# Moving the subtractions that GpSimd did outside the expert stages to VectorE, in a two-block transformer kernel

## The chip, the cores and the metric

The kernel runs on one core of a Trainium2 chip. A core has five engines that run side by side, each with a queue of its own that it works off strictly in order: TensorE (PE in the profile, with PEld for the loading of its stationary operand), VectorE (DVE), ScalarE (ACT), GpSimd (POOL) and SyncE (SP, which here only issues transfers). They wait for each other by semaphores. Sixteen DMA engines move data between HBM and the on-chip memory SBUF; matrix products land in the accumulators of PSUM. The metric is the time of one execution on the device, in microseconds, lower is better.

## The reference

256 tokens of width 1024 pass through two blocks, all in float32. The lines that matter, in the order in which the kernel computes them:

```python
# first block, layer 0: mLSTM, layer 1: multi-head latent attention (MLA)
x = layer_norm(DN_ALPHA * x + mix, ln_g[i, 0], ln_b[i, 0])          # mix = mlstm_mixer or mla_mixer
x = layer_norm(DN_ALPHA * x + peer_ffn(x, ...), ln_g[i, 1], ln_b[i, 1])   # expert stage: 16384 experts, top 16 of 8 heads
x = x + sigmoid(x @ ple_w_gate[i]) * (p[i] @ ple_w_proj[i])          # gated addition ("c0", "c1" in the kernel)
...
# second block
h = modulate(rmsnorm(x, norm_mix_g[l]), sh1, sc1)
x = x + g1 * hybrid_mixer(h, ...)     # sparse attention (8 heads) + stick-breaking attention (8 heads), merged by gates
h = modulate(rmsnorm(x, norm_ffn_g[l]), sh2, sc2)
x = x + g2 * swiglu(h, ...)           # silu(h @ w_gate) * (h @ w_up) @ w_down
return rmsnorm(x, norm_final_g)
```

Inside `mlstm_mixer` the gates go through running sums and running maxima over the tokens; inside `mla_mixer` and `hybrid_mixer` there are softmax steps per head. `peer_ffn` scores all keys, takes the best 16 experts per head and token and adds up their weighted outputs.

## The kernel before

**How a product is made.** Activations lie transposed, features on the 128 partitions and the 256 tokens along the row. Each float32 product is built of three products of a shorter type, called by `mm3` (L159 to L161): every operand is cut into a high part `hi` (the value copied to the short type) and a low part `lo` (the value less `hi`). L159 multiplies hi by hi, L160 and L161 the two mixed pairs. So each weight has to be split before it can be used, and a low part is an operation with two inputs in SBUF.

**How weights come.** `prep` loads one slab of 1 MB (128 partitions x 2048 values) into one of 3 `raw` buffers by a transfer issued on SP. It is split in two halves; `split` (its two lines are L128 and L129) issues for each half a copy `hi` on ScalarE (shown under L78, the helper for all ScalarE work; 8 buffers) and a subtraction `lo` (L129; 7 buffers). The argument `lo_engine` says who does the subtraction: VectorE if it is missing, GpSimd where the caller passes `nc.gpsimd`. A `raw` buffer is free for the next transfer when both halves are split, a `lo` buffer when TensorE has done the last product that reads it. `slab` calls `prep` where that hasn't been done; `linT` and `linN` multiply by all slabs of a matrix, giving the result transposed or not.

**Who subtracted before.** In the page, 634 subtractions of weights stand on VectorE and 120 on GpSimd. Those of GpSimd are 40 in the expert stages (in `peer` and the look-ahead loads there) and 80 outside them: the value, output-gate and output matrices of the mLSTM layer (`a_w_v`, `a_w_og`, half of `a_w_out`), every second slab of the gated additions (`ple_w_gate`), the MLA projections (`mla_kn`, `mla_v`, `mla_uq`, `b_w_out`), the eight slabs of `merge`, and a few first slabs of other matrices. GpSimd also does two splits of 128x512 (`pre`), one product `trig` (L961), four masked products in the stick-breaking attention (L1302), eight additions (L1350), a scaling of 128x1024 (L435), and in `post_norm` 48 subtractions of 128x128 (L276).

**The stages**, by the time in the span of the profiled execution: mLSTM 0 to 145 us, norm and expert scoring 145 to 247, expert stage 247 to 980, gated addition c0 with its norm 980 to 1027, MLA 1027 to 1130, norm and scoring 1130 to 1210, second expert stage 1210 to 1965, c1 to 2023, hybrid attention to 2230, its output projection to 2290, feed-forward to the end.

**What sets the order.** The program is written as straight Python; a framework orders the instructions of every engine by a model of their durations, and puts in the semaphores. So where a subtraction stands in VectorE's queue is the scheduler's choice, and whatever stands behind it waits if it waits. `behind` and `issue_after` only hold pieces of work back until a named instruction is issued.

**The places named further down.** In the mLSTM layer L464 to L469 make the gates' running sums on VectorE (32x256), L481 transposes them on TensorE, and L482 copies the result. L221 to L228 (`rsqrt` by two refinement steps, tiny operands) serve every norm; L340 and L342 spread its result over the partitions. In c0 and c1, L853 and L854 form `(tanh + 1) * p` and add it to `x`; then c0 splits `x` (lines L128, L129, tile `s`) and transposes it (L871), and c1 takes squares (L320) and scaled copies (L372) for the next norm, whose sum is L330. In the MLA heads L896 to L898 make scores, softmax is L988 (maximum), an exponential on ScalarE, L993 and L995 (dividing), L1004 transposes, L905 multiplies by the values. L997 is the same step as L995 in the hybrid attention.

Of the kernel before, what the change touches and what calls it, by code (L numbers as in the profile page):

```python
# [17 lines left out]
OP = mybir.AluOpType  # L18
# [4 lines left out]
P = 128  # L23
# [324 lines left out]
class Modulated:  # L348
# [28 lines left out]
    def finish(self, name, evac):  # L377

        B, v = self.B, self.B.nc.vector
        self.rms.col()  # L380
        rs = self.rms.bc()
        ws = B.slab(name, 0, B.nc.gpsimd)
        ps = [B.psum("acc") for _ in range(2)]
        for k in range(KD):
            for j in range(2):
                B.mm3(ps[j][:, 0:S + 2], ws(k, j * P, (j + 1) * P), (self.hi[:, k, :], self.lo[:, k, :]),
                      k == 0, k == KD - 1)
        for k in range(KD):
            t = B.t(self.pool, [P, S], F32, "hm", bufs=3)
            sh = B.mod[:, self.o + k:self.o + k + 1]  # L390
            g = B.mod[:, self.o + KD + k:self.o + KD + k + 1]
            hi, lo = (a[:, k, :] for a in B.xT)
            v.scalar_tensor_tensor(t, B.x32[:, k, :], g, rs, op0=OP.mult, op1=OP.mult)
            i_act = B.act(hi, t, AF.Identity, bias=sh)
            i_dve = v.scalar_tensor_tensor(lo, t, sh, hi.bitcast(F32), op0=OP.add, op1=OP.subtract)
        B.last = (i_act.ins, i_dve.ins)
        for j in range(2):
            t = B.t(self.pool, [P, S], F32, "hm", bufs=3)
            col = B.t(B.small, [P, 1], F32, "wsh")
            v.tensor_copy(col, ps[j][:, S:S + 1])  # L400
            v.tensor_tensor(t, ps[j][:, 0:S], rs, op=OP.mult)
            evac(j, t, col)
# [11 lines left out]
def mlstm(B):  # L414
    nc, A = B.nc, B.A
    mm = nc.tensor.matmul
    v = nc.vector
    act = B.act
    with B.pool("ml") as p, B.pool("mlw", 2) as w:
        for n, i in (("a_w_gate", 0), ("a_w_qk", 0)):  # L420
            B.prep(n, i, nc.gpsimd if i else v)
        nc.sync.dma_start(B.X, A["x"])
# [61 lines left out]
        act(flo, tok[:, :, 32:40], AF.Exp, scale=-1.0)  # L484
        acc = B.linN(B.xT, "a_w_v", lo_engine=nc.gpsimd)
        for tb in range(2):
# [62 lines left out]
        for h in range(8):  # L549
            if h < 7:  # L550
                head_a(h + 1)
            for i in gates[h]:
                hf, k = i // 8, i % 8
                ws = B.slab("a_w_og", k // 4 * 2 + hf, nc.gpsimd) if k % 4 == 0 else ws
                for tb in range(2):
# [11 lines left out]
            if h in (6, 7):  # L567
                B.accN(acc, [(oT, B.slab("a_w_out", h - 6, nc.gpsimd), 2 * h - 12, 2)], h == 6, False)
        norm_heads(1)
        B.warm()  # L570
        B.accN(acc, [(oT, B.slab("a_w_out", s), 2 * s, 2) for s in (2, 3)], False, True)
        with B.pool("rows") as rows:
            B.prep("peer_w_q", 0, nc.gpsimd)
            B.post_norm(acc, 0, rows)
# [251 lines left out]
def norm_ple(B, acc, li, pre, pre_p):  # L826

    nc, A = B.nc, B.A
    v = nc.vector
    act = B.act  # L830
    with B.pool("plew", 2) as w:
# [3 lines left out]
        nc.sync.dma_start(p32, A["pT"][li])  # L835
        B.split(p32, *pT, nc.gpsimd)
        B.prep("ple_w_proj", li, nc.gpsimd)
        if acc:
# [23 lines left out]
        with B.behind():  # L862
            B.linT(B.xT, "ple_w_gate", range(li * 4, li * 4 + 4), ev, lambda s: nc.gpsimd if s % 2 else v,
                   k_outer=True, base=li * 8)
# [10 lines left out]
def mla(B):  # L875
# [5 lines left out]
    with B.pool("mla") as p, B.pool("mlaw", 2) as w, ExitStack() as ctx2:  # L881
# [44 lines left out]
        def w_out(s):  # L926
            B.accN(acc, [(oT, B.slab("b_w_out", s, nc.gpsimd), 2 * s, 2)], s == 0, False)

        with B.pool("lat") as lt:
# [26 lines left out]
            rkb = rk.bc()  # L956
            B.linT(ckT, "mla_kn", [0], lambda c, ps: v.tensor_tensor(kn[:, c, :], ps, rkb, op=OP.mult), nc.gpsimd)
            rq.col()
            rqb = rq.bc(192.0 ** -0.5)
            trig = B.t(lt, [P, S], F32, "trig")  # L960
            nc.gpsimd.tensor_tensor(trig, B.trig, rqb, op=OP.mult)  # L961
            acc = B.linN(ckT, "mla_v", nc.gpsimd)
            for tb in range(2):
# [9 lines left out]

            heads(lambda s: B.linT(cqT, "mla_uq", [s], ev_q, nc.gpsimd))
        B.warm()
        B.accN(acc, [(oT, B.slab("b_w_out", s, nc.gpsimd), 2 * s, 2) for s in (2, 3)], False, True)
        with B.pool("rows") as rows:
            B.prep("peer_w_q", 8, nc.gpsimd)
            B.post_norm(acc, 2, rows)
# [64 lines left out]
def hybrid(B):  # L1044
# [5 lines left out]
    with B.pool("hy") as p, B.pool("hyw", 2) as w, ExitStack() as es:  # L1050
# [37 lines left out]
        nc.sync.dma_start(w2, A["w2"])  # L1088
        B.linT(hT, "nsa_in", [1], ev_a, nc.gpsimd, k_outer=True)
        with B.behind():  # L1090
# [151 lines left out]
        ob = (B.t(p2, [P, 4, S], F32R, "obh"), B.t(p2, [P, 4, S], F32R, "obl"))  # L1242
        merge = lambda i: B.linT(hT, "merge", [i], lambda c, ps: v.tensor_copy(mg[:, c, :], ps), nc.gpsimd)

# [47 lines left out]
        def stick_sp(i):  # L1292
# [8 lines left out]
            for o in (0, S):  # L1301
                nc.gpsimd.tensor_tensor(ab[:, :, o:o + P], ab[:, :, o:o + P],  # L1302
                                        sm.unsqueeze(1).to_broadcast([P, 4, P]), op=OP.mult)
# [43 lines left out]
        def ev_yb(c, ps):  # L1347
            t = B.t(w, [P, S], F32, "vT")
            v.scalar_tensor_tensor(t, mg[:, 8 + c, :], 1.0, ps, op0=OP.add, op1=OP.mult)
            nc.gpsimd.tensor_tensor(t, mg[:, c, :], t, op=OP.add)  # L1350
            act(hT[0][:, c, :], t, AF.Copy, scale=0.5)
# [20 lines left out]
def ffn(B, out):  # L1372
    nc, A, v = B.nc, B.A, B.nc.vector
    with B.pool("ff") as p, B.pool("ffw", 2) as w:
# [18 lines left out]
        rms = Rms(B, p, RMS_EPS)  # L1393
        B.linT(hT, "ffn_up", [0], ev_u, nc.gpsimd, k_outer=True)
        for s in range(1, NF // 2):
# [182 lines left out]
```

## Time and profile before

| | |
|---|---|
| median of three runs | 2478.57 us (2474.83 to 2481.1) |
| the profiled execution, its own time | 2474.93 us |
| its span, first to last instruction | 2472.0 us |
| TensorE busy | 2373.6 us, 96% of the span, mean granted clock 0.981 |
| VectorE busy | 1627.4 us, 66% |
| ScalarE busy | 1230.4 us, 50% |
| GpSimd busy | 346.4 us, 14% in 212 instructions |

Busy time counts what an engine executes, from the start to the end that the profiler recorded. It does not tell waiting inside an instruction from working: an instruction that is held up while it runs has a longer duration, and looks busy. So durations of the same operation and shape are to be compared with each other. "Idle before" is time in which the engine stood still, and the releaser is what ended it. A granted clock of 1.00 is 2.4 GHz, 0.50 is 1.2 GHz.

### The profile page before, as it was taken

What the parts mean: (1) busy time and instruction counts of PE and PEld (TensorE: products, weight loads), DVE (VectorE), ACT (ScalarE), POOL (GpSimd) and SP (SyncE); (2) the same over time, 40 slices, a digit from 0 to 9 for tenths busy, and PEclk for the clock granted to TensorE, in tenths of its full rate; (3) what the DMA queues carried; (4) which work ended last, traced back from release to release, by engine and by line L of the source; (5) the groups of instructions that cost most, each with busy time, mean ns of one, the idle gap of its engine ahead of it and who ended that gap; (6) DMA issues with size and microseconds to landing.
All of it is one profiled execution on the core that took longest, in us unless ns stands there. A gap on an engine that the chain in (4) does not pass through costs nothing. (4 is left out here: it accounts for less than half of the span.)

```text
span 2472.0 us, 40796 instructions
## 1 busy us (share of the span) xinstructions
PE 2373.6 (96%) x16430; PEld 2167.0 (88%) x16430; DVE 1627.4 (66%) x3069; ACT 1230.4 (50%) x1813; POOL 346.4 (14%) x212
## 2 busy tenths in 40 slices
PE   7989999999999999989989999999999989999998
PEld 6779898889999998978989888999999888789998
DVE  5469995786666665656999566555555573459554
ACT  5455555444444444645455444444444464455442
POOL 5345000000000001445300000000000131313000
PEclk9989999999999999999999999999999999999999
DMA  7334577887677664433367766656655344224543
GB/s 258 120 110 150 226 282 268 293 326 264 251 263 273 255 227 148 154 137 131 144 239 280 258 236 218 227 200 208 218 208 201 137 162 160 81 86 161 198 149 108
DMA packets 134204, 495.22 MB, mean 200 GB/s; under 512 B 8064, under 2 KB 76032, under 8 KB 80896
## 3 DMA queue, kind: packets, MB, share of 16 engines
q1 hardware_dynamic: 129120, 458.55, 51.8%
q10 hardware_dynamic: 4896, 34.08, 3.4%
q8 instruction: 128, 2.10, 0.3%
q14 instruction: 60, 0.49, 0.1%
HBM read 457.99 MB, written 34.60 MB: 199 GB/s over the span
## 5 line engine op out<-in xcount | busy, mean ns | idle before, releaser
L78 ACT ACTIVATE hi<-raw 128x1024 fp32r<-128x1024 f32 (+1 forms) x754 | 771.3, 1044 | 838.8 <-PE ps L160 336.8
L129 DVE TENSOR_TENSOR lo<-raw,hi 128x1024 fp32r<-128x1024 f32 (+1 forms) x634 | 778.0, 1234 | 420.6 <-PE ps L161 254.2
L159 PE MATMUL ps<-s,hi 128*128 128x256 f32 x3248 | 923.5, 285 | 16.3 <-ACT hi L78 13.8
L160 PE MATMUL ps<-s,hi 128*128 128x256 f32 x3248 | 924.2, 285 | 2.1 <-DVE s L276 1.5
L161 PE MATMUL ps<-s,lo 128*128 128x256 f32 x3248 | 921.0, 284 | 5.3 <-DVE lo L129 5.3
L159 PEld LDWEIGHTS ps<-s,hi 128*128 128x128 f32 x3248 | 617.4, 190 | 22.6 <-ACT hi L78 14.2
L160 PEld LDWEIGHTS ps<-s,hi 128*128 128x128 f32 x3248 | 618.3, 190 | 7.4 <-issue 2.2
L161 PEld LDWEIGHTS ps<-s,lo 128*128 128x128 f32 x3248 | 617.9, 190 | 7.3 <-DVE lo L129 7.3
L129 POOL TENSOR_TENSOR lo<-raw,hi 128x1024 fp32r<-128x1024 f32 (+1 forms) x120 | 292.4, 2455 | 1340.6 <-ACT hi L78 1148.9
L159 PE MATMUL acc<-hi,ah 128*128 128x512 f32 x1024 | 400.6, 391 | 9.6 <-ACT ah L78 9.5
L160 PE MATMUL acc<-lo,ah 128*128 128x512 f32 x1024 | 401.0, 392 | 0.0
L161 PE MATMUL acc<-hi,al 128*128 128x512 f32 x1024 | 400.1, 391 | 0.0
L159 PEld LDWEIGHTS acc<-hi,ah 128*128 128x128 f32 x1024 | 193.1, 189 | 49.1 <-ACT ah L78 10.8
L161 PEld LDWEIGHTS acc<-hi,al 128*128 128x128 f32 x1024 | 193.0, 189 | 41.2 <-DVE al L129 0.7
L160 PEld LDWEIGHTS acc<-lo,ah 128*128 128x128 f32 x1024 | 193.0, 188 | 37.9
L129 DVE TENSOR_TENSOR al<-aw,ah 128x512 fp32r<-128x512 f32 x128 | 88.2, 689 | 54.9 <-ACT ah L78 54.8
L78 ACT ACTIVATE ah<-aw 128x512 fp32r<-128x512 f32 x128 | 80.1, 626 | 71.3 <-DVE aw L789 62.5
L789 DVE TENSOR_TENSOR aw<-g,wt 128x256 f32<-128x256 f32 x156 | 59.3, 422 | 39.4 <-ACT g L78 39.4
L756 PE MATMUL ps<-oh,o 128*128 128x128 f16 x512 | 65.1, 219 | 11.5 <-DVE oh L750 5.0
L78 ACT ACTIVATE st<-ps 128x512 f32<-128x512 f32 x128 | 66.6, 604 | 1.6 <-ACT pre L78 1.6
L78 ACT ACTIVATE g<-ps 128x512 f32<-128x512 f32 (+1 forms) x82 | 46.5, 567 | 39.1 <-PE ps L161 39.1
L757 PE MATMUL ps<-ol,o 128*128 128x128 f16 x512 | 64.7, 218 | 0.0
(461 smaller groups left out, 2433.6 us busy)
## 6 DMA issues: line engine op xcount, KB each, us to landing
raw<-in_peer_u SPq DMA_DIRECT2D x128, 1024.0 KB, 4.9
raw<-in_peer_v SPq DMA_DIRECT2D x128, 1024.0 KB, 4.9
wd<-st ACTq DMA_DIRECT2D x32, 1024.0 KB, 4.5
wt<-wd SPq DMA_DIRECT2D x32, 1024.0 KB, 6.1
raw<-in_w_ada SPq DMA_DIRECT2D x24, 1024.0 KB, 5.3
raw<-in_peer_w_q SPq DMA_DIRECT2D x16, 1024.0 KB, 4.9
raw<-in_ffn_gate SPq DMA_DIRECT2D x11, 1024.0 KB, 4.8
raw<-in_ffn_up SPq DMA_DIRECT2D x11, 1024.0 KB, 4.8
```

Source lines behind the costliest of these rows:

```text
L78: i = self.nc.scalar.activation(out, in_, func, **kw)
L129: (lo_engine or self.nc.vector).tensor_tensor(lo, src, hi.bitcast(F32), op=OP.subtract)
L159: mm(out, lhsT[0], rhs[0], start=first, stop=False)
L160: mm(out, lhsT[0], rhs[1], start=False, stop=False)
L161: mm(out, lhsT[1], rhs[0], start=False, stop=last)
L756: mm(ps[:, i * P:(i + 1) * P], o2[:, t // 2, :, t % 2], oh1[:, t // 2, :, t % 2], start=True, stop=False)
L757: w_last = mm(ps[:, i * P:(i + 1) * P], o2[:, t // 2, :, t % 2], ol1[:, t // 2, :, t % 2], start=False, stop=True)
L789: v.tensor_tensor(aw[:, sl].rearrange("p (g t) -> p g t", t=16), g[:, sl].rearrange("p (g t) -> p g t", t=16), wt[:, :, (j % 4) * 2 + i, : ...
```

## The change

Wherever a caller outside the expert stages asked for GpSimd, the argument is dropped, so that VectorE does the subtraction; the operations on GpSimd at L961, L1302 and L1350 are issued on VectorE too. GpSimd keeps what `peer` and its look-ahead give it, the 48 operations of `post_norm` (L276), the scaling at L435, and masks and counters that read nothing. The diff, cut to its core (`prep`, `slab`, `linT`, `linN` and `split` are the same as before):

```diff
-        ws = B.slab(name, 0, B.nc.gpsimd)
+        ws = B.slab(name, 0)
...
-            B.prep(n, i, nc.gpsimd if i else v)
+            B.prep(n, i)
...
-        acc = B.linN(B.xT, "a_w_v", lo_engine=nc.gpsimd)
+        acc = B.linN(B.xT, "a_w_v")
...
-                ws = B.slab("a_w_og", k // 4 * 2 + hf, nc.gpsimd) if k % 4 == 0 else ws
+                ws = B.slab("a_w_og", k // 4 * 2 + hf) if k % 4 == 0 else ws
...
-                B.accN(acc, [(oT, B.slab("a_w_out", h - 6, nc.gpsimd), 2 * h - 12, 2)], h == 6, False)
+                B.accN(acc, [(oT, B.slab("a_w_out", h - 6), 2 * h - 12, 2)], h == 6, False)
...
-            B.prep("peer_w_q", 0, nc.gpsimd)
+            B.prep("peer_w_q", 0)
...
-        B.split(p32, *pT, nc.gpsimd)
-        B.prep("ple_w_proj", li, nc.gpsimd)
+        B.split(p32, *pT)
+        B.prep("ple_w_proj", li)
...
-            B.linT(B.xT, "ple_w_gate", range(li * 4, li * 4 + 4), ev, lambda s: nc.gpsimd if s % 2 else v,
+            B.linT(B.xT, "ple_w_gate", range(li * 4, li * 4 + 4), ev,
                    k_outer=True, base=li * 8)
...
-            B.linT(ckT, "mla_kn", [0], lambda c, ps: v.tensor_tensor(kn[:, c, :], ps, rkb, op=OP.mult), nc.gpsimd)
+            B.linT(ckT, "mla_kn", [0], lambda c, ps: v.tensor_tensor(kn[:, c, :], ps, rkb, op=OP.mult))
...
-            nc.gpsimd.tensor_tensor(trig, B.trig, rqb, op=OP.mult)
-            acc = B.linN(ckT, "mla_v", nc.gpsimd)
+            v.tensor_tensor(trig, B.trig, rqb, op=OP.mult)
+            acc = B.linN(ckT, "mla_v")
...
-            heads(lambda s: B.linT(cqT, "mla_uq", [s], ev_q, nc.gpsimd))
+            heads(lambda s: B.linT(cqT, "mla_uq", [s], ev_q))
...
-        merge = lambda i: B.linT(hT, "merge", [i], lambda c, ps: v.tensor_copy(mg[:, c, :], ps), nc.gpsimd)
+        merge = lambda i: B.linT(hT, "merge", [i], lambda c, ps: v.tensor_copy(mg[:, c, :], ps))
...
-                nc.gpsimd.tensor_tensor(ab[:, :, o:o + P], ab[:, :, o:o + P],
+                v.tensor_tensor(ab[:, :, o:o + P], ab[:, :, o:o + P],
...
-            nc.gpsimd.tensor_tensor(t, mg[:, c, :], t, op=OP.add)
+            v.tensor_tensor(t, mg[:, c, :], t, op=OP.add)
```

The same argument also goes at `b_w_out` (four slabs), `peer_w_q` slab 8, `nsa_in` slab 1 and `ffn_up` slab 0. In all, 80 weight subtractions (72 of 128x1024, 8 of 128x768) and 15 other operations change their engine. In numbers: 22 of the subtractions lie in the mLSTM layer, 28 in c0 and MLA, 10 in c1, 20 in the hybrid attention and after it.

Where they stand now is the scheduler's doing. First VectorE's queue in the mLSTM layer, where the gates' running sums end (`lo_497` to `lo_565` are low parts of `a_w_v`, `tok` the copies after the transposes of L481):

```order
 L468 TENSOR_TENSOR Bc_240<-Bc_240,M_243 32x256
 L469 COPY ab_48_238<-Bc_240 32x256
+L129 TENSOR_TENSOR lo_497<-raw_494,hi_496 128x1024
+L129 TENSOR_TENSOR lo_501<-raw_494,hi_500 128x1024
+L129 TENSOR_TENSOR lo_531<-raw_528,hi_530 128x1024
+L129 TENSOR_TENSOR lo_535<-raw_528,hi_534 128x1024
+L129 TENSOR_TENSOR lo_565<-raw_562,hi_564 128x1024
 L482 COPY tok_481<-ps_482 128x64
 L482 COPY tok_481<-ps_485 128x64
```

Five of the subtractions stand behind the last step of the running sums and ahead of the copies; none stands among the steps themselves.

Second VectorE's queue in MLA, ahead of the heads, where the norm of the query latents is finished (`lo_11000` and `lo_11111` are low parts of `mla_uq`, 128x768):

```order
 L957 TENSOR_TENSOR kn_10452<-ps_10744,rsk_10687 128x256 x2
+L129 TENSOR_TENSOR lo_11000<-raw_10993,hi_10999 128x768
 L221 TENSOR_SCALAR rmqh_10765<-ps_10759 128x2
 L222 RECIPROCAL rmq_10764<-rmq_10764 128x2
+L129 TENSOR_TENSOR lo_11111<-raw_11108,hi_11110 128x768
 L226 TENSOR_TENSOR rmqh_10765<-rmqh_10765,rmq_10764 128x2
 L227 TENSOR_TENSOR rmqh_10765<-rmqh_10765,rmq_10764 128x2
 L228 SCALAR_TENSOR_TENSOR rmq_10764<-rmqh_10765,rmq_10764 128x2
 L340 TENSOR_SCALAR dgq_10772<-ident_79,rmq_10764 128x128 x2
```

Here a subtraction now stands in the middle of the chain that ends in L340.

Third VectorE's queue in c1, among the gate steps (`lo_20472` to `lo_20584` and `lo_20700` belong to `ple_w_gate` and the first slabs of the hybrid attention):

```order
+L129 TENSOR_TENSOR lo_20472<-raw_20469,hi_20471 128x1024
 L372 SCALAR_TENSOR_TENSOR s_3196_20235<-x_17_117,mod_108,s_3195_20234 128x256
 L320 TENSOR_TENSOR sqs_20302<-sqs_20302,sq_20310 128x256
 L372 SCALAR_TENSOR_TENSOR s_3196_20235<-x_17_117,mod_108,s_3195_20234 128x256
+L129 TENSOR_TENSOR lo_20476<-raw_20469,hi_20475 128x1024
+L129 TENSOR_TENSOR lo_20580<-raw_20577,hi_20579 128x1024
 L853 SCALAR_TENSOR_TENSOR sg_20374<-sg_20374,pre_1862_11564 128x256
 L853 SCALAR_TENSOR_TENSOR sg_20383<-sg_20383,pre_1862_11564 128x256
 L854 TENSOR_TENSOR x_17_117<-x_17_117,sg_20374 128x256
 L854 TENSOR_TENSOR x_17_117<-x_17_117,sg_20383 128x256
+L129 TENSOR_TENSOR lo_20584<-raw_20577,hi_20583 128x1024
 L320 TENSOR_TENSOR sqs_20302<-sqs_20302,sq_20378 128x256
```

Subtractions now stand between the pairs of gate steps. SP's queue of transfers is the same in both kernels.

## Rows read from the trace of the kernel before

**Rows 1.** The page: busy time, share of the span, instructions of each engine.

```profile
PE 2373.6 (96%) x16430; PEld 2167.0 (88%) x16430; DVE 1627.4 (66%) x3069; ACT 1230.4 (50%) x1813; POOL 346.4 (14%) x212
```

**Rows 2.** Instructions of L129: duration in ns min/median/max, first and last start, forms.

```profile
L129 DVE TENSOR_TENSOR lo<-raw,hi x634: 818/1225/3425, 10.6 to 2448.5; 128x1024 fp32r<-128x1024 f32 x151, 128x768 fp32r<-128x768 f32 x8
...
L129 POOL TENSOR_TENSOR lo<-raw,hi x120: 1795/2403/3930, 35.4 to 2257.6; 128x1024 fp32r<-128x1024 f32 x112, 128x768 fp32r<-128x768 f32 x8
...
L129 DVE TENSOR_TENSOR s<-x,s x16: 409/422/2591, 5.2 to 1026.1; 128x256 fp32r<-128x256 f32 x16
```

**Rows 3.** Waits of PE over the run: us in total, times, longest us.

```profile
PE acc L159 <- ACT s L78: 5.2, 1, 5.2
...
PE acc L871 <- DVE x L854: 3.8, 2, 2.1
...
PE ps L481 <- POOL lo L129: 3.4, 1, 3.4
PE ps L330 <- DVE sqs L320: 3.1, 2, 2.9
PE ps L342 <- DVE dgq L340: 2.9, 1, 2.9
...
PE ps L896 <- ACT e L78: 2.3, 1, 2.3
PE ps L540 <- ACT sg L78: 2.3, 1, 2.3
PE ps L905 <- ACT pT L78: 2.1, 2, 1.7
```

**Rows 4.** Stretches: length, busy PE, PEld, DVE, ACT, POOL, PEclk, DMA share, GB/s.

```profile
930.00:1150.00 220.00, 201.19 (x1318) 181.68 (x1318) 131.12 (x244) 117.97 (x222) 84.22 (x58) 0.95 0.36 131
```

**Rows 5.** Timeline, mLSTM gates: start us, us, engine, line, out<-in [idle before <-releaser].

```profile
36.43 0.67 DVE L464 TENSOR_TENSOR_SCAN Bc<-lf,zero 32x256 f32<-32x256 f32 x1
37.14 2.44 DVE L465 TENSOR_TENSOR ab<-ig,Bc 32x256 f32<-32x256 f32 x1
39.61 2.77 DVE L467 TENSOR_TENSOR_SCAN M<-ab,zero 32x256 f32<-32x256 f32 x1
...
44.88 2.31 DVE L469 COPY ab<-Bc 32x256 f32<-32x256 f32 x1
```

**Rows 6.** Timeline of POOL, 35 to 53 us.

```profile
35.37 18.75 POOL L129 TENSOR_TENSOR lo<-raw,hi 128x1024 fp32r<-128x1024 f32 x7 [5.70 <-DVE lf L458]
```

**Rows 7.** The stretch right after PE's wait at L481, columns as in Rows 4.

```profile
47.70:51.10 3.40, 3.40 (x9) 2.66 (x10) 0.23 (x2) 2.11 (x3) 3.40 (x2) 0.50 0.82 299
```

**Rows 8.** Timeline of DVE, 128 to 136 us.

```profile
132.64 2.32 DVE L227 TENSOR_TENSOR hrh<-hrh,hr 128x8 f32<-128x8 f32 x1
```

**Rows 9.** Timeline of DVE, end of c0.

```profile
1021.63 2.59 DVE L129 TENSOR_TENSOR s<-x,s 128x256 fp32r<-128x256 f32 x1
```

**Rows 10.** Timeline of DVE and ACT, norm ahead of the MLA heads.

```profile
1056.31 1.72 DVE L227 TENSOR_TENSOR rmqh<-rmqh,rmq 128x2 f32<-128x2 f32 x1
...
1056.50 0.83 ACT L78 ACTIVATE hi<-raw 128x768 fp32r<-128x768 f32 x1
```

**Rows 11.** Timeline of DVE, MLA heads.

```profile
1073.03 2.07 DVE L995 TENSOR_SCALAR e<-e,sm 128x256 f32<-128x256 f32 x1
...
1078.99 0.36 DVE L995 TENSOR_SCALAR e<-e,sm 128x256 f32<-128x256 f32 x1
```

**Rows 12.** Timeline of DVE, c1.

```profile
1996.18 4.05 DVE L853 SCALAR_TENSOR_TENSOR sg<-sg,pre 128x256 f32<-128x256 f32 x2 [1.65 <-ACT sg L78]
2000.15 2.95 DVE L854 TENSOR_TENSOR x<-x,sg 128x256 f32<-128x256 f32 x2
...
2012.95 0.75 DVE L853 SCALAR_TENSOR_TENSOR sg<-sg,pre 128x256 f32<-128x256 f32 x2
```

**Rows 13.** Waits of POOL, 1062 to 1130 us, columns as in Rows 3.

```profile
POOL lo L129 <- PE ps L161: 9.8, 5, 4.4
```

**Rows 14.** Waits of POOL, 2060 to 2230 us.

```profile
POOL lo L129 <- PE ps L161: 101.5, 9, 57.0
```

More of the change, by code (lines that the diff above doesn't have):

```diff
@@ L926, in w_out @@
         def w_out(s):
-            B.accN(acc, [(oT, B.slab("b_w_out", s, nc.gpsimd), 2 * s, 2)], s == 0, False)
+            B.accN(acc, [(oT, B.slab("b_w_out", s), 2 * s, 2)], s == 0, False)
         with B.pool("lat") as lt:
@@ L972, in ev_q @@
                 v.tensor_tensor(qn[c // 4][:, c % 4, :], ps, trig if c % 2 else rqb, op=OP.mult)
-            heads(lambda s: B.linT(cqT, "mla_uq", [s], ev_q, nc.gpsimd))
+            heads(lambda s: B.linT(cqT, "mla_uq", [s], ev_q))
         B.warm()
-        B.accN(acc, [(oT, B.slab("b_w_out", s, nc.gpsimd), 2 * s, 2) for s in (2, 3)], False, True)
+        B.accN(acc, [(oT, B.slab("b_w_out", s), 2 * s, 2) for s in (2, 3)], False, True)
         with B.pool("rows") as rows:
-            B.prep("peer_w_q", 8, nc.gpsimd)
+            B.prep("peer_w_q", 8)
             B.post_norm(acc, 2, rows)
@@ L1088, in hybrid @@
         nc.sync.dma_start(w2, A["w2"])
-        B.linT(hT, "nsa_in", [1], ev_a, nc.gpsimd, k_outer=True)
+        B.linT(hT, "nsa_in", [1], ev_a, k_outer=True)
         with B.behind():
@@ L1393, in ffn @@
         rms = Rms(B, p, RMS_EPS)
-        B.linT(hT, "ffn_up", [0], ev_u, nc.gpsimd, k_outer=True)
+        B.linT(hT, "ffn_up", [0], ev_u, k_outer=True)
         for s in range(1, NF // 2):
```

## The prediction

> **What bounds the kernel now.** First the engine line [rows 1]: TensorE is busy for 2373.6 of the 2472.0 us of the span, VectorE for 66%, GpSimd for 14%. So the end is set by TensorE, and a change on other engines counts only where TensorE stands still for them, or runs at half clock after standing still. All of its idle time is 98.4 us. Then the waits of TensorE [rows 3], which are the places where something can be won. Eight of them lie in stages where GpSimd subtracts: L481 3.4, L540 2.3, L871 3.8 (two waits), L342 2.9, L896 2.3, L905 2.1, L159 behind a scaled copy 5.2, L330 3.1; together 25.1 us. All are for VectorE or for ScalarE behind it, but for L481, where the view names GpSimd.
>
> Then the durations, since a busy VectorE may be a held-up one. In the mLSTM layer a running sum of 32x256 takes 0.67 us at 36.43, and the running maximum of the same size 2.77 at 39.61; the steps around it, no larger, take 2.44 and 2.31 [rows 5]. GpSimd is subtracting without a pause from 35.37 to 54.1 [rows 6]. The same shows everywhere: L227 on 128x8 takes 2.32 [rows 8], a split of 128x256 2.59 [rows 9] with a median of 0.42 over 16 [rows 2], L995 2.07 and six us later 0.36 [rows 11], a pair of L853 4.05 and later 0.75 [rows 12]. The long ones are as long as one subtraction on GpSimd, whose median is 2.40 [rows 2]: the two engines do not share, one is shut out until the other has finished. It goes both ways, GpSimd's longest subtraction is 3.93 and VectorE's 3.42 [rows 2].
>
> The Trainium skill says the same on "SBUF — State Buffer", § Who interferes with whom: an instruction of VectorE with two inputs in SBUF is locked out for the whole of a GpSimd instruction that reads SBUF, and the other way round, by who begins first; the rows above agree.
>
> **The change part by part.**
>
> What moves: 80 weight subtractions. On VectorE the median is 1.225 us [rows 2], so 72 of 128x1024 cost 88 us; the 8 of 768 take about three quarters, 0.9 each, 7 us. The 15 others, by their sizes, come to some 9 us. So VectorE gets about 104 us of work. What goes are the held-up instructions. Each costs about what [rows 8, 9, 11, 12] show, 1.7 to 2.2 us more than its own time; I count some fifty in the trace, the first of them at 37.14 [rows 5], 80 us in all, of which about 70 in the stages where the change takes GpSimd's work away. So VectorE's busy time rises by only some 30 us, to about 1660, and in place of long steps there are short ones with subtractions between them. In total that is little; what counts is which stand ahead of the steps that TensorE waits for.
>
> A. L481 (wait 3.4). The chain of the four steps ends at 44.88 + 2.31 = 47.19 [rows 5]. Free of GpSimd each takes at most the 0.67 of the first, so from 37.14 it ends by 39.8, before TensorE comes to the transposes (47.3 less the wait of 3.4, 43.9). The five subtractions stand behind the chain and not in it; they end by 39.8 + 5 x 1.22 = 45.9, and for each of them TensorE has twelve products of 512 columns to do, of which nine took 3.40 us at half clock [rows 7], so at least 2.3 at full clock; the other subtractions follow in time. The whole wait goes, and no later step takes its place. Behind it TensorE ran 3.40 us at half clock, busy all the time [rows 7]; with no idle stretch ahead I count that back too, 1.7. **-5.1 us**, bounds -3.4 and -5.1.
>
> B. L540 (2.3). L227 loses 2.15. But `lo_1229` now stands between L226 and L227 and costs 1.22, and it waits for a `lo` buffer that TensorE is reading until about then. L226 comes earlier, since the first step of that chain was held up too. **-1.1**, bounds 0 and -2.3.
>
> C. L871 in c0 (3.8). Of the second wait (2.1) the 2.59 for a split of 0.42 [rows 9] is the whole cause. The first hangs on a ScalarE copy whose load came late, since its `raw` buffer was kept by a subtraction on GpSimd (2.4 instead of 1.2). The gated slabs' four subtractions join VectorE's queue ahead of the pairs L853, L854; one waits for a `lo` buffer. I take three quarters, -3, and 1 for half clock behind it. **-4**, bounds -1 and -5.5.
>
> D. L342 (2.9). L227 loses 1.5 [rows 10]. But `lo_11111` stands between L222 and L226 now, 0.96 us long, and its high part comes from ScalarE only at 1056.50 + 0.83 = 1057.33 [rows 10], behind a copy there that itself waits for TensorE. So L226 starts at 1058.3 and L340 ends where it did or later. **+0.5**, bounds -1.5 and +1.2.
>
> E. MLA heads, L896 and L905 (4.4 in all). Both waits end behind an L995 held up by 1.7 [rows 11]. Eleven subtractions (13 us) enter the queue here, against about 11 us of hold-ups that go, and some stand right ahead of an L993 or L995. **-2**, bounds -4.4 and +4.
>
> F. c1, L159 and L330 (5.2 and 2.9 in one row). From 1996 the pairs take 4.05 and 2.95 instead of 0.75 each [rows 12], the next pair of L853 again some 4; with the two subtractions before them (one of 3.42) that is about 11.5 us of hold-ups. Eight subtractions enter ahead of the last pair, 9.8 us, of which some 4 fit where VectorE stood idle for ScalarE (1.65 before the pair, [rows 12], once more before the next). 11.5 - 5.8 = 5.7 at best; two copies now stand in ScalarE's queue behind a load, so I take **-4.4**, bounds -1 and -8 (with clock, -9).
>
> G. Nothing for the rest. Hybrid attention: three held-up L997 go, 16 subtractions come; TensorE's waits there sum to under 4 us in the whole stage, since its many small products keep it busy, so 0, bounds -2 and +3. Output projection and feed-forward: TensorE has no wait of a us that ends with VectorE; its cover is TensorE's own work of 256-column products, and gone it would cost the eight L1350 at some 0.4 each, 3 us. `pre` and `trig` lie where VectorE idles. Expert stages and `post_norm` are as before. Transfers start a little earlier, as `raw` buffers come free in 1.2 instead of 2.4 us; TensorE does not wait for loads in these stages, so 0.
>
> Sum: -5.1 - 1.1 - 4 + 0.5 - 2 - 4.4 = **-16.1 us**. The profiled execution took 2474.93 us (span 2472.0 and 2.9 around it), so 2458.8. It lies at the low end of the three runs; from the median of 2478.57 the same sum gives 2462.5. I say 2460.
>
> A rule that speaks against the change is in the Trainium skill, "Perfetto Trace Analysis", § Optimizing Scalar/DVE Operations: where VectorE is saturated, giving work to GpSimd may make sense. By it VectorE would become the bound; the share in [rows 4], 131.12 of 220 us, is 60%, part of it waiting, so the row does not show the saturation that it asks for. The same section adds that it may not help between these two engines because of the shared port, which is what the durations above show.
>
> **The rivals.**
>
> 1. *The queue takes back what the lock gives.* VectorE works strictly in order; wherever a subtraction stands ahead of a step that TensorE waits for, 1.2 us of it replace 1.7 to 2.1 of hold-up. Then only A and B remain, with D against them, and C, E, F are zero: -5.7, or 2469 to 2473. For it: eleven, eight and four subtractions enter E, F, C. Against: half of them fit in VectorE's idle time.
>
> 2. *Slower: VectorE inherits GpSimd's waits for `lo` buffers.* GpSimd stood 9.8 us in five waits for TensorE to release a buffer in the MLA heads [rows 13] and 101.5 in nine in the hybrid attention [rows 14], with nobody behind it. On VectorE the softmax steps stand behind such a wait. If the 9.8 and the shorter five of the nine (14 us in sum) reach TensorE, they take back 23.8, +7.7 net: about 2483 to 2486. It decides from the point where a subtraction is queued more than a us before its buffer is released and L988 or L995 is next. For it: `lo` has 7 buffers, all full there. Against: the scheduler places the subtractions late, after several steps of a head.
>
> 3. *More comes back.* If the waits of C, E and F go whole and TensorE keeps full clock behind them, -5.1 - 2.3 - 5.5 - 4.4 - 9 = -26: 2449 to 2452.
>
> 4. *It isn't GpSimd that holds VectorE up.* Then the long durations stay, 104 us are added, and A gets 6 us longer: about 2485. Against: each long step lies beside a GpSimd instruction and none without one.
>
> **How the numbers follow.** Forecast 0.54, rival 1 0.19, rival 2 0.10, rival 3 0.14, rival 4 0.03. A measurement of this kernel tells some 0.3% (7.4 us) from no change. Against the median that is 2471.1: the forecast and rival 3 lie below, and of rival 1 about a quarter; faster 0.73. Same 0.16: the rest of rival 1 and the mild end of rival 2. Slower 0.11. The range leaves out rivals 2 and 4 and the far end of 3: 2449 to 2475.
>
> **What would show it.** In the profile after: four steps L464 to L469 under 0.7 us each and no wait at L481; no L853, L995 or L227 over 1 us outside the expert scoring; subtractions on GpSimd 40; VectorE busy 1640 to 1680; the waits of L871 and of L159 for a scaled copy under 1 and 4 us; L342's wait about 3. The prediction is wrong if new waits of TensorE for L988, L995 or L997 appear behind subtractions that wait for TensorE (rival 2), or if TensorE's idle time stays near 98 us while the steps are short (rival 1).

## The result and the profile after

The changed kernel takes 2439.2 us (median of 6 runs, 2436.3 to 2447.5), the kernel before in the same series 2479.84: ratio 0.9842, 95% interval 0.982 to 0.9864, some 40 us or 1.6% less. In a second series it took 2442.68 against 2478.72, 0.9852 (0.9833 to 0.9872). The direction was as forecast, the size was not: the prediction's sum was 16.1 us and its time 2460 us, and 2439 lies 10 us below the low end of the range.

The engine line of the page of the changed kernel, against [rows 1], and the L129 rows of the view by lines, against [rows 2] (duration in ns min/median/max):

```profile
PE 2354.2 (97%) x16430; PEld 2152.7 (88%) x16430; DVE 1655.3 (68%) x3164; ACT 1231.7 (51%) x1813; POOL 134.2 (6%) x117
```

```profile
L129 DVE TENSOR_TENSOR lo<-raw,hi x714: 820/1225/3409, 10.1 to 2410.9; 128x1024 fp32r<-128x1024 f32 x169, 128x768 fp32r<-128x768 f32 x10
...
L129 POOL TENSOR_TENSOR lo<-raw,hi x40: 2368/2398/3372, 156.6 to 1182.9; 128x1024 fp32r<-128x1024 f32 x40
L129 DVE TENSOR_TENSOR s<-x,s x16: 417/422/428, 5.0 to 1010.4; 128x256 fp32r<-128x256 f32 x16
```

80 subtractions are gone from GpSimd, and VectorE is busy for 28 us more, not for the 104 us of its new work: the rest was made up of instructions that had been held up. The split `s`, which had a maximum of 2.59 us, now has one of 0.43. The gates' chain shows the same (timeline of VectorE, against [rows 5]): 0.67, 0.41, 0.68, 0.41 and 0.28 us, done at 39.3 instead of 47.2. The copy L469 has a single input and was held up like the others (2.31 us, now 0.28), and so was L995 with one tensor and one value per partition [rows 11]; so it was not only steps with two inputs. Of the steps of VectorE that take over 1 us more than the median of the same operation and shape in the changed kernel, the kernel before has 39 and the changed one 4, all subtractions in the expert scoring, where GpSimd still works.

```profile
36.73 0.67 DVE L464 TENSOR_TENSOR_SCAN Bc<-lf,zero 32x256 f32<-32x256 f32 x1
37.44 0.41 DVE L465 TENSOR_TENSOR ab<-ig,Bc 32x256 f32<-32x256 f32 x1
37.88 0.68 DVE L467 TENSOR_TENSOR_SCAN M<-ab,zero 32x256 f32<-32x256 f32 x1
...
39.04 0.28 DVE L469 COPY ab<-Bc 32x256 f32<-32x256 f32 x1
```

TensorE's waits over the whole run (us in total, times, longest), against [rows 3]. Of the 25.1 us of eight waits four small ones are left; L481, L896, L330 and the 5.2 us at L159 no longer appear.

```profile
PE ps L342 <- DVE dgq L340: 2.1, 1, 2.1
...
PE ps L905 <- ACT pT L78: 1.2, 1, 1.2
PE ps L540 <- ACT sg L78: 1.1, 1, 1.1
...
PE acc L871 <- DVE x L854: 0.2, 1, 0.2
```

That is 20.5 us, and the span is shorter by 37.7. Where the other half is can be read from windows that are cut at the same products of both kernels (columns as in [rows 4]: length, busy PE, PEld, DVE, ACT, POOL with counts, granted clock, DMA). First the kernel before: mLSTM; c0 with the beginning of MLA; the heads; c1; the hybrid attention with its output projection.

```profile
0.00:151.01 151.01, 130.83 (x658) 105.74 (x658) 76.56 (x171) 75.50 (x127) 61.13 (x36) 0.95 0.47 169
...
982.80:1055.48 72.68, 65.71 (x501) 63.46 (x499) 45.01 (x82) 50.01 (x95) 36.84 (x26) 0.95 0.40 145
1055.48:1129.37 73.89, 66.38 (x388) 56.37 (x386) 39.47 (x93) 31.20 (x71) 29.12 (x15) 0.95 0.32 114
...
1967.19:2021.80 54.61, 43.30 (x309) 42.30 (x307) 38.80 (x67) 33.29 (x72) 28.35 (x29) 0.84 0.42 156
2021.80:2272.82 251.02, 244.97 (x1724) 213.37 (x1723) 146.48 (x315) 130.66 (x253) 64.18 (x33) 0.97 0.33 120
```

The same five in the changed kernel:

```profile
0.00:140.35 140.35, 123.56 (x657) 100.35 (x658) 85.41 (x193) 75.54 (x127) 6.56 (x14) 1.00 0.49 182
...
972.16:1039.84 67.68, 64.25 (x501) 62.38 (x499) 49.27 (x95) 50.43 (x95) 5.58 (x12) 0.97 0.43 156
1039.84:1108.85 69.01, 65.69 (x388) 56.14 (x386) 41.24 (x107) 31.39 (x71) 0.24 (x1) 0.95 0.34 123
...
1946.58:1989.24 42.66, 39.44 (x309) 38.54 (x307) 33.94 (x75) 33.37 (x72) 6.94 (x21) 0.96 0.47 177
1989.24:2235.26 246.02, 240.32 (x1724) 210.49 (x1723) 157.55 (x347) 131.05 (x253) 0.34 (x1) 0.99 0.34 126
```

The stages are shorter by 10.7, 5.0, 4.9, 12.0 and 5.0 us, 37.5 in sum; the windows left out, with the expert stages, norms and feed-forward, differ by 0.14 us at most. Idle time of TensorE (length less busy) falls by 3.4, 3.5, 4.2, 8.1 and 0.4 us, 19.6 in sum. Its busy time falls as well, by 7.3, 1.5, 0.7, 3.9 and 4.7 us, 17.9 in sum, with as many products. Products that take less time with the same shapes are products at a higher clock, and the column of the granted clock says so in four of the five: 0.95 to 1.00, 0.95 to 0.97, 0.84 to 0.96, 0.97 to 0.99. So about half of this profile's gain is time that TensorE no longer waits, and half is clock. The prediction had 13.4 for the one and 2.7 for the other. How much of this belongs to this one profile is taken up below.

### The profile page after: what moved, and what is told of

Read it like the earlier page. It is cut to its first block, busy times and chain, and to the rows that moved or that the text cites. A ratio compares the mean times of both kernels' runs of the same rounds, so it can differ in the third digit from the quotient of the medians.

```text
span 2434.3 us, 40711 instructions
## 1 busy us (share of the span) xinstructions
PE 2354.2 (97%) x16430; PEld 2152.7 (88%) x16430; DVE 1655.3 (68%) x3164; ACT 1231.7 (51%) x1813; POOL 134.2 (6%) x117
## 4 chain that ended last, share of the span: by engine, by line
PE 47%; DVE 1%; ACT 1%; DMA 1%; issue 0%; DVEq 0%; SPq 0%; ACTq 0%
PE ps L160 9%; PE ps L161 9%; PE ps L159 9%; PE acc L159 5%; PE acc L160 5%; PE acc L161 5%; PE ps L1258 1%; PE acc L1271 0%; DMA wt<-wd 0%; PE ps L756 0%; PE acc L1144 0%; DVE lo L129 0%; PE ps L757 0%; PE ps L1259 0%; PE ps L1004 0%
## 5 line engine op out<-in xcount | busy, mean ns | idle before, releaser
L129 DVE TENSOR_TENSOR lo<-raw,hi 128x1024 fp32r<-128x1024 f32 (+1 forms) x714 | 865.4, 1219 | 456.6 <-PE ps L161 269.5
L159 PE MATMUL ps<-s,hi 128*128 128x256 f32 x3248 | 921.5, 285 | 15.9 <-ACT hi L78 13.3
L159 PEld LDWEIGHTS ps<-s,hi 128*128 128x128 f32 x3248 | 615.4, 190 | 22.1 <-ACT hi L78 13.7
L159 PE MATMUL acc<-hi,ah 128*128 128x512 f32 x1024 | 401.1, 392 | 10.3 <-ACT ah L78 10.2
L159 PEld LDWEIGHTS acc<-hi,ah 128*128 128x128 f32 x1024 | 193.4, 189 | 49.6 <-ACT ah L78 11.5
L160 PEld LDWEIGHTS acc<-lo,ah 128*128 128x128 f32 x1024 | 193.2, 189 | 37.7
L129 DVE TENSOR_TENSOR al<-aw,ah 128x512 fp32r<-128x512 f32 x128 | 88.3, 690 | 55.4 <-ACT ah L78 54.6
L276 POOL TENSOR_TENSOR s<-x,s 128x128 fp32r<-128x128 f32 x48 | 24.3, 520 | 1545.9 <-ACT x L78 1533.2
L129 POOL TENSOR_TENSOR lo<-raw,hi 128x1024 fp32r<-128x1024 f32 x40 | 98.3, 2476 | 23.4 <-PE ps L161 12.8
```

Of the source, the lines that this page charges most:

```text
L129: (lo_engine or self.nc.vector).tensor_tensor(lo, src, hi.bitcast(F32), op=OP.subtract)
L159: mm(out, lhsT[0], rhs[0], start=first, stop=False)
L160: mm(out, lhsT[0], rhs[1], start=False, stop=False)
L276: lo = (v if tb and k % 2 == 0 else nc.gpsimd).tensor_tensor(xT[1][:, k, ts], x32[:, k, ts], xT[0][:, k, ts].bitcast(F32), op=OP.subtract)
```

## Experiments

**Is it the lock, or only the quicker subtraction?** Theory A: a GpSimd operation that reads SBUF shuts VectorE out. Rival B: 1.22 instead of 2.40 us a subtraction is the gain. Two kernels have the subtractions on VectorE and then let GpSimd work beside it for nothing; in one it reads, in the other it mostly writes. They differ from the kernel before in this (`in_peer` is true inside `peer`):

```diff
-        (lo_engine or self.nc.vector).tensor_tensor(lo, src, hi.bitcast(F32), op=OP.subtract)
+        g = self.nc.gpsimd
+        beside = lo_engine is g and not self.in_peer
+        (self.nc.vector if beside else lo_engine or self.nc.vector).tensor_tensor(lo, src, hi.bitcast(F32), op=OP.subtract)
+        if beside:
+            l = lo.bitcast(F32)
```

In dve_pool_read this is followed by an operation of the same size into a spare buffer `scr`:

```diff
+            o = self.scr[:, 0:l.shape[1] * l.shape[2]].rearrange("p (k n) -> p k n", n=l.shape[2])
+            g.tensor_tensor(o, l, l, op=OP.subtract)
```

In dve_pool_write by a copy of one column and zeros:

```diff
+            g.tensor_copy(self.scr[:, 0:1], l[:, 0, 0:1])
+            for _ in range(3):
+                g.memset(self.scr[:, 0:896], 0.0)
```

L961, L1302, L1350 and the split of 128x512 stand on VectorE in both, and `hi` has 7 buffers instead of 8. The twelve subtractions of c0 and c1 stayed on GpSimd in both, other than the expectation says, since these stages are called from within `peer`; 68 of the 80 were moved and shadowed.

> All subtractions and the other moved operations stand on VectorE as in the changed kernel, but after each of the moved weight subtractions GpSimd reads the low part twice and writes the difference to a buffer that nobody uses (80 operations of the size of the old ones; 7 hi buffers instead of 8 to make room). Theory A (a GpSimd operation that reads SBUF shuts VectorE out, and TensorE waits for the held-up steps): some 30 or more steps of VectorE again over 1 us longer than their own time, VectorE busy 60 us or more above the changed kernel's 1655, the waits at L871 and at L159 for a scaled copy back, 2460 to 2485 us. Rival B (the gain is that a subtraction takes 1.22 instead of 2.40 us, so that low parts and raw buffers are ready earlier): the subtractions are as fast as in the changed kernel, 2436 to 2446 us.

Measured: 2474.8 us, ratio to the kernel before 0.9992 (0.9984 to 1.0001).

> The same as dve_pool_read, with the same order on VectorE, ScalarE and TensorE, but GpSimd copies one element per partition and then writes zeros three times (128x896), as long in sum and with hardly any reading. Theory A: few held-up steps, 2436 to 2448 us, and at least 15 us below dve_pool_read. Rival B: as dve_pool_read, both within 5 us. Rival C (any work of GpSimd hinders VectorE): as slow as dve_pool_read, both over 2460.

Measured: 2449.71 us, ratio 0.9889 (0.9873 to 0.9905). The first line below is the engine line of dve_pool_read, the second that of dve_pool_write, each from its page.

```profile
PE 2369.8 (96%) x16430; PEld 2164.6 (88%) x16430; DVE 1702.2 (69%) x3152; ACT 1234.6 (50%) x1813; POOL 311.8 (13%) x197
```

```profile
PE 2367.1 (97%) x16430; PEld 2161.6 (88%) x16430; DVE 1646.6 (67%) x3152; ACT 1235.0 (50%) x1813; POOL 363.2 (15%) x401
```

GpSimd is busier in the second, and the second is 25 us faster. VectorE executes the same 3152 instructions in both, and is busy for 55.6 us more where GpSimd reads; both traces have the mean clock 0.982, and their spans differ by 21.0 us (2472.6 and 2451.6), so the clock is not the difference there. By the count used above, 45 steps of VectorE are held up in the first and 10 in the second, these ten all in c0, c1 and the expert scoring, where GpSimd still subtracts. In c1 the pairs of L853 (here on lines 867 and 868, since lines were added) take 2.45 us beside a reading GpSimd and 0.75 beside a writing one (timeline of VectorE of the first, then of the second):

```profile
1996.07 2.45 DVE L867 SCALAR_TENSOR_TENSOR sg<-sg,pre 128x256 f32<-128x256 f32 x2
```

```profile
1991.39 0.75 DVE L868 SCALAR_TENSOR_TENSOR sg<-sg,pre 128x256 f32<-128x256 f32 x2
```

Rival B falls, though not by the total alone: in the mLSTM layer of dve_pool_read fifteen subtractions on VectorE are held up themselves (1.8 to 2.9 us). In the MLA heads eleven of twelve are as quick as in the changed kernel, and yet the stage takes 74.8 us beside a reading GpSimd and 69.5 beside a writing one, against 73.9 in the kernel before and 69.0 in the changed one (windows, cut at the same products as above, of the first and of the second):

```profile
1046.88:1121.66 74.78, 65.40 (x387) 55.23 (x386) 51.53 (x107) 32.29 (x72) 24.90 (x15) 0.95 0.31 115
```

```profile
1049.13:1118.62 69.49, 64.50 (x388) 54.88 (x386) 45.27 (x107) 32.20 (x72) 39.63 (x56) 0.98 0.34 124
```

Rival C falls too, that any work of GpSimd hinders. dve_pool_write lies just above the range expected by theory A, 9 to 12 us slower by the ratios than the changed kernel. That fits the twelve subtractions that stayed on GpSimd, the single-element copies and the buffer less; which of them it is wasn't tried apart.

**Does the clock fall because TensorE stood still?** Theory D. In the kernel before, TensorE waits 3.4 us at L481 and then runs 3.4 us at half clock [rows 7]. fill_l481 leaves the wait and fills it:

```diff
-            ps = B.psum()
+            ps = B.psum(); [mm(ps[:, P:2 * P], B.ident_b, B.cmask_b, start=True, stop=True) for _ in range(0 if tb else 56)]
             nc.tensor.transpose(ps[:, :64], ab2[:, tb * P:(tb + 1) * P], B.ident[:64, :64])
```

> The kernel before with 56 products of 128 columns, whose result is overwritten, ahead of the transposes of L481, where TensorE waits 3.4 us. They take 56 x 0.056 = 3.1 us, less than the wait, so the wait's end stays where it is. Theory D (the clock falls because TensorE stood still): no half clock at 47.7 to 51.1, the end 1.7 us earlier, or more if the later stretch at 75 goes too. Rival E (half clock comes from elsewhere): half clock stays there, the time as before, 2480.

Measured: 2475.43 us, ratio 0.9987 (0.9977 to 0.9998). The windows of its trace at the place of [rows 7] (the first us still holds the last of the additional products), and further on:

```profile
47.70:51.10 3.40, 3.40 (x31) 2.89 (x29) 1.12 (x3) 1.77 (x2) 3.40 (x3) 1.00 0.48 157
75.00:81.80 6.80, 6.80 (x19) 4.75 (x19) 0.61 (x2) 0.47 (x2) 0.58 (x2) 0.54 0.32 135
```

The clock stays at 1.00 behind the filled wait, and the gain of 2.7 us (interval 0.5 to 5.7) agrees with 1.7. But this place alone shows nothing: in only_hybrid and only_c0_mla, described below, the mLSTM code is that of the kernel before, TensorE waits 3.2 us at L481 with no filling, and the clock behind is 1.00 as well (windows right behind the wait, of the one and of the other):

```profile
48.30:51.70 3.40, 3.40 (x15) 2.80 (x16) 0.28 (x2) 2.12 (x3) 3.40 (x2) 1.00 0.82 284
```

```profile
49.40:52.80 3.40, 3.40 (x15) 2.77 (x16) 0.25 (x2) 2.12 (x3) 3.40 (x2) 1.00 0.83 296
```

In these two traces and in that of fill_l481 a stretch of 3.4 us at half clock stands at 26 to 27 us, where the first profile of the kernel before has none. The half clock at 75 stays; no wait of a us stands ahead of it, and it follows small products (L499 to L501, on 8 and 64 partitions). So there are half-clock stretches that no wait explains, and waits that none follows.

The same was tried on the changed kernel, at the four layer norms (L263) and ahead of the second half of each expert stage (L765):

```diff
-                ps[tb, h] = self.psum()
+                ps[tb, h] = self.psum(); [nc.tensor.transpose(ps[tb, h][:, 0:P], Y[:, 0, 7 * P:8 * P], self.ident) for _ in range(22 if tb and not h else 0)]
```

fill_both has this as well:

```diff
-        acc = [[B.psum("acc") for _ in range(2)] for _ in range(2)]
+        acc = [[B.psum("acc") for _ in range(2)] for _ in range(2)]; [nc.tensor.transpose(acc[0][0][:, 0:P], pre[NPRE - 2][:, 0:P], B.ident) for _ in range(36)]
```

> The changed kernel, with 22 additional transposes of 128x128 (their result is overwritten) in each of the four layer norms, between the transposes of the first and the second half of the tokens, where TensorE waits 2.8 to 3.1 us for VectorE (L260). 22 x 0.11 = 2.4 us, so they fit. In the changed kernel 6.8, 3.4, 6.8 and 3.4 us at half clock follow these waits. Theory D (half clock follows standing still, and costs half of its length): the waits stay as long, but the clock behind them is 1.00, 8 to 10 us less than the changed kernel's 2439: 2429 to 2432. Rival E (the clock falls there for another reason): half clock stays, 2438 to 2442.

Measured: 2436.86 us, ratio 0.9831 (0.9817 to 0.9844).

> As fill_norm2, and 36 such transposes (4.0 us) ahead of the second half of each expert stage, where TensorE waits 6.0 and 4.5 us for a transfer; there 6.8 and 3.4 us at half clock follow. Theory D: 3 to 5 us less than fill_norm2, 2424 to 2428. Rival E: as the changed kernel, or slower by what of the transposes doesn't fit.

Measured: 2432.73 us, ratio 0.9826 (0.981 to 0.9841). To see it beside the changed kernel, both ran once more on one chip:

> The changed kernel itself, beside fill_both_again on the same chip. Theory D says that about half of its gain is clock: mean granted clock 0.986 to 0.990 in every run against 0.977 to 0.983 of the kernel before, 2436 to 2447 us, though the profiled execution may show other stretches at half clock than the first one did, some of them in the mLSTM layer, where the first had none. If the clock of the first profile was luck, the clocks spread down to 0.982 and the median is 2445 or more.

Measured: 2442.68 us (2439.46 to 2446.68), clocks 0.985 to 0.988.

> The kernel of fill_both once more, beside the changed kernel. Theory D: 4 to 8 us less than after_again and a clock at least 0.002 higher. If the additional transposes cost what the clock gives: within 3 us of after_again.

Measured: 2435.54 us (2431.93 to 2436.37), clocks 0.990 to 0.993, 7.1 us below the changed kernel beside it; ratio to the kernel before 0.9824 (0.981 to 0.9838). Its interval overlaps that of after_again by a little, but in the two series together eight of its ten runs lie below all ten of the changed kernel. It is the fastest version here, and does nothing but more work.

The clock behind the norms, in the changed kernel and in fill_norm2 (windows):

```profile
143.60:150.40 6.80, 5.79 (x25) 5.24 (x26) 5.17 (x16) 6.13 (x16) 3.33 (x9) 0.50 0.00 0
976.50:979.90 3.40, 3.40 (x18) 3.40 (x18) 2.23 (x8) 2.90 (x9) 2.38 (x6) 0.50 0.00 0
```

```profile
145.00:152.00 7.00, 5.29 (x40) 4.33 (x39) 5.65 (x18) 6.92 (x21) 3.48 (x9) 1.00 0.00 0
976.00:983.00 7.00, 6.64 (x51) 5.63 (x50) 4.89 (x15) 6.88 (x17) 2.96 (x6) 1.00 0.01 2
```

At the third norm 3.4 of the 6.8 us stay in fill_norm2, at the fourth none. Added up over 20 us from the first transposes of each of the four norms, the twelve traces without this filling have 20 to 27 us at half clock, the three with it 3.4, 6.8 and 6.8. So at these places theory D is shown. In the whole time less came of it: 2 and 7 us where 8 to 10 and 11 to 15 were expected, and fill_norm2 alone can't be told from the changed kernel. Other half-clock stretches had come up, in fill_norm2 at 70 and at 132 us, where the code is that of the changed kernel. The second profile of the changed kernel itself shows two there as well. Its span and mean clock, and its engine line, against those of the first profile (2434.3 us, 0.989, PE 2354.2):

```profile
core 0: 2442.4 us, clock 0.985
```

```profile
PE 2362.3 (97%) x16430; PEld 2159.3 (88%) x16430; DVE 1655.4 (68%) x3164; ACT 1232.0 (50%) x1813; POOL 134.2 (5%) x117
```

The same program, the same waits of L342, L905 and L540, and 8.1 us longer; TensorE's busy time is longer by the same 8.1 us, and no other engine's by more than 0.3. Where half clock falls changes from run to run. The five windows, cut at the same products, in the second profile:

```profile
0.00:145.64 145.64, 129.78 (x657) 105.78 (x658) 84.98 (x193) 75.38 (x127) 6.67 (x14) 0.95 0.49 175
...
981.22:1048.57 67.35, 63.96 (x501) 62.12 (x499) 49.31 (x95) 50.57 (x95) 5.58 (x12) 0.97 0.43 157
1048.57:1114.98 66.41, 63.09 (x388) 53.65 (x386) 41.24 (x107) 31.40 (x71) 0.24 (x1) 1.00 0.35 127
...
1951.89:1994.52 42.63, 39.26 (x308) 38.36 (x307) 33.94 (x75) 33.38 (x72) 6.92 (x21) 0.96 0.48 178
1994.52:2243.34 248.82, 243.11 (x1725) 212.54 (x1723) 157.83 (x347) 131.14 (x253) 0.35 (x1) 0.97 0.34 125
```

Against the kernel before, TensorE's idle time falls by 20.4 us here and by 19.6 in the first profile: that part is steady. The busy time falls by 12.0 instead of 17.9; the mLSTM layer is 5.4 us shorter and not 10.7, c1 again 12.0. The first profile of the changed kernel was a lucky one, the lowest of its six runs.

**Do the stages add up?** Four kernels make the change in one stage each.

> The kernel before with the change in the mLSTM layer alone (22 subtractions: a_w_qk's, a_w_v, a_w_og, a_w_out, peer_w_q slab 0). If the stages add up, it gains what the changed kernel's trace had gained by the norm after this layer: about 10 us, so 2468; by the prediction's sum for this layer alone 6. If a gain in one stage is given back in the next, under 3.

Measured: 2466.34 us, ratio 0.9954 (0.9938 to 0.997).

> The kernel before with the change in c0 and MLA alone (28 subtractions, one split of 128x512, trig). Adding up: about 10 us, so 2468; by the prediction's terms C, D, E 5.5. If VectorE's queue takes it back there: 0 to 2.

Measured: 2463.72 us, ratio 0.9931 (0.9909 to 0.9954).

> The kernel before with the change in c1 and the first slabs of the hybrid attention alone (10 subtractions, one split). Adding up: about 11 us, so 2467; by the prediction's term F 4.4.

Measured: 2465.38 us, ratio 0.9942 (0.9926 to 0.9958).

> The kernel before with the change in the hybrid attention and after alone (20 subtractions: merge, first slabs of the feed-forward; L1302 and L1350). Adding up: about 5 us, so 2473; by the prediction 0. If what the changed kernel won there was only where its half-clock stretches fell, the gain is within 2 us of nothing.

Measured: 2474.85 us, ratio 0.9988 (0.9971 to 1.0005), not to be told from no change.

By the ratios the gains are 11.4, 17.1, 14.4 and 3.0 us; their sum of 46 is as much as the 36 to 40 of the whole change, given that each is uncertain by 4 to 6. So the stages add up within this, and rival 1 of the prediction, by which C, E and F come to nothing, falls. Only only_c0_mla gained clearly more than was expected (10). In only_c1 the stage itself is within a us of the changed kernel's, 43.65 us instead of 54.61, with 3.2 us instead of 11.3 of idle time, though the whole run's clock is only 0.980:

```profile
1978.66:2022.31 43.65, 40.42 (x309) 39.71 (x307) 33.96 (x75) 33.55 (x72) 6.93 (x21) 0.92 0.47 173
```

Each stage stands in its old form in five of the traces (the kernel before, fill_l481 and three of these four) and in its new form in five others (the two profiles of the changed kernel, peer_dve, norm_dve and the fourth). Cut at the same products, in us:

| stage | length, old form | length, new form | of it at half clock, old | new |
|---|---|---|---|---|
| mLSTM | 151.0 to 154.3 | 139.5 to 145.6 | 13.7 to 17.1 | 0 to 13.7 |
| c0, start of MLA | 72.7 to 75.3 | 67.3 to 67.7 | 6.8 to 13.7 | 3.4 |
| MLA heads | 73.7 to 74.1 | 66.4 to 69.1 | 6.8 | 0 to 6.8 |
| c1 | 54.2 to 54.6 | 42.4 to 43.6 | 13.7 to 17.1 | 3.4 to 6.8 |
| hybrid attention | 245.2 to 251.0 | 244.4 to 249.2 | 3.4 to 17.1 | 3.5 to 13.7 |

The means differ by 9.7, 6.2, 6.5, 11.6 and 0.9 us, 34.9 in sum. So the gain of the first four stages is steady, and that of the hybrid attention in the first pair of profiles was where half clock happened to fall.

**Moving the rest.** peer_dve moves the 40 subtractions of the expert stages (`lambda s: v if s % 8 < 3 else nc.gpsimd` and the `nc.gpsimd` of `ahead` dropped), norm_dve the 48 of L276.

> The changed kernel with the 40 subtractions of the expert stages on VectorE too, so that GpSimd keeps only post_norm's and masks. Theory A alone would give back the four subtractions of 3.4 us that are still held up and the wait of 1.7 us behind them: 2433 to 2438. Against it, VectorE is busy for 57 of 67 us of the expert scoring and gets 24 us more in each of the two, where it searches the best 16; then TensorE waits for it there and the time is 2445 to 2460.

Measured: 2455.88 us, ratio 0.991 (0.9896 to 0.9924), 14 to 17 us slower by the ratios than the changed kernel. The new waits, at the end of the second expert scoring (waits of TensorE, 1195 to 1225 us; 6.0 in two waits stand in the first):

```profile
PE ps L161 <- DVE lo L129: 7.6, 2, 4.1
```

There VectorE searches for the best 16, and the subtraction stands behind it. That is the limit of the rule: by the count above no step of VectorE is held up any more, and yet the time is longer.

> The changed kernel with the 48 subtractions of 128x128 in the layer norms (L276) on VectorE too, which is busy in these stages. Theory A: the one step of L286 held up by 0.3 us in each of two norms gets shorter and each L276 falls from 0.5 to about 0.3, but 12 x 0.3 us queue on VectorE in each norm, ahead of steps that TensorE waits for: 2437 to 2445. If VectorE isn't what TensorE waits for there: 2434 to 2439.

Measured: 2441.82 us, ratio 0.9853 (0.9837 to 0.987), the same as the changed kernel.

## Why the prediction was wrong

Its mechanism was right and is shown: the lock (dve_pool_read against dve_pool_write), the places where it costs TensorE something, the busy time of VectorE (1655.3 us, 1640 to 1680 was said); rivals 1, 2 and 4 did not come true. The sum was too small by more than half. Two of its terms were mis-sized. The clock was put at 2.7 us, and TensorE's busy time fell by 17.9 and 12.0 us in the stages concerned. The idle time that goes was put at 13.4 us, and 19.6 and 20.4 went; of the 6 to 7 us missing, 3.7 are F's and most of the rest D's and E's. By its own steps:

- **A** (-5.1). Right. In the changed kernel and in only_mlstm the products after the transposes of L481 come 5.0 us earlier against those ahead of them than in the kernel before (the same products matched in the traces), in the second profile too. That the 1.7 us of clock in it follow from the wait is not shown: the wait is there in only_hybrid and only_c0_mla without them. The layer won 9.7 us in the mean, 3.5 more than A and B together; its half-clock stretches at other places are gone in three of the five traces of its new form and there in the two others. The chain ended at 39.3, 39.8 was said.
- **B** (-1.1). Right: L540 waits 1.1 instead of 2.3.
- **C** (-4). Right in kind, 3.6 of the 3.8 us of waits are gone, not 3; the stage is 5.0 shorter.
- **D** (+0.5). Wrong in sign: L342 waits 2.1 instead of 2.9. The subtraction in the chain costs 0.94 us, less than the held-up steps did, and it did not wait: the last copy on ScalarE ahead of it had ended at 1039.40, and it began at 1040.36, where the prediction had it wait for its high part.
- **E** (-2). Too small: the wait of L896 is gone, that of L905 is 1.2 instead of 2.1, TensorE's idle time in the window falls by 4.2, 0.8 of it by D's wait.
- **F** (-4.4). The stage that failed most, by 7.6 us: it is 12.0 us shorter in both profiles, 8 us idle and 4 us clock. Its step was that eight subtractions of 1.22 us would be paid for except in 4 us of idle time, so that 3.7 of the 8.1 us of waits stay. None stays. VectorE's own account in the window shows both halves of the error: its busy time falls by 4.9 us although 9.8 us of subtractions come, so 14.7 us of hold-ups went and not 11.5, and its idle time falls by 7.1 us (15.8 to 8.7), not 4. The account looked at VectorE alone, and left out that ScalarE, too, had stood behind it. Waits of ScalarE in c1, before and after (us, times, longest):

```profile
ACT sq L78 <- DVE x L854: 9.6, 2, 5.4
ACT sqs L78 <- DVE x L854: 4.5, 1, 4.5
```

```profile
ACT sg L78 <- PE ps L161: 4.2, 3, 2.5
...
ACT sq L78 <- DVE x L854: 1.2, 1, 1.2
```

  14.1 us of waiting for L854 came down to 1.2, and what ScalarE now waits for is TensorE. That the waits of the two engines had come from each other in a circle is an argument that fits these rows; it wasn't tried apart. With the steps short the last pair of L853 finds VectorE idle for 1.58 us ahead of it:

```profile
1982.59 0.76 DVE L853 SCALAR_TENSOR_TENSOR sg<-sg,pre 128x256 f32<-128x256 f32 x2 [1.58 <-ACT sg L78]
```

- **Clock.** It was counted at two places, 2.7 us, and left to the range in the others. The busy time of TensorE fell by 17.9 us in the five windows of the first profile and by 12.0 in the second. In c1 it is steady: the stage has 13.7 to 17.1 us at half clock in all five traces of its old form and 3.4 to 6.8 in those of the new, where the waits are gone. Elsewhere some of it isn't bound to a wait: the stretch at 75 us was not behind one, and in the second profile 8.1 us of the whole fall were gone again. Taken over all runs, the mean clock is 0.977 to 0.983 in the 23 runs of the kernel before of one series, and 0.985 to 0.990 in the ten of the changed kernel, so most of it stays. What share of that follows from the waits and what from other shifts of the work remains open.
- **G** (0). Right as far as is shown. The hybrid attention is 5.0 us shorter in the first profile, 4.7 of it clock, but its old form takes 245.2 to 251.0 us and its new one 244.4 to 249.2, and only_hybrid can't be told from no change.
- **Rival 3** (more comes back, 2449 to 2452, a chance of 0.14) was the right case in the main, though half of B's wait and part of E's stayed, and its own number was still 10 us too high. It had F at 9 us for 12.0, and counted no clock in the mLSTM layer beyond L481 and none in the heads.

## What to carry over

Where VectorE has short steps on SBUF in a chain that TensorE waits for, long operations on GpSimd that read SBUF beside them can cost more than their own length on VectorE would; look in the trace for the same operation and shape with two durations, and for what runs on GpSimd during the long one. Move them, unless VectorE has a long search of its own ahead of them (peer_dve). And look at a wait of TensorE twice: at the idle time, and at the granted clock of the stretch behind it. The second price does not come with every wait (none in two traces behind 3.2 us at L481, 13.7 to 17.1 us of half clock in c1 in every trace of its old form), so take it from more than one profile.

## What the runs showed that was not expected

Additional products that do nothing made the kernel faster, 2435.54 against 2442.68 us on the same chip, by filling waits of TensorE that stayed as they were. And two profiles of one program differ by 8.1 us through where half clock falls; a stage's gain that is read from one profile (10.7 us in mLSTM, 5.4 by the second) is uncertain by several us even where the waits of that stage hardly differ.
